# The two gates of a recurrent block: from two block-diagonal products to two products in row halves

## The chip, the cores and the metric

The kernel runs on one core of a Trainium2 chip. The metric is the time on the device of one execution, in microseconds, as the median of the runs shown. The core has a matrix engine (TensorE, PE in the profile), two engines for element-wise work (VectorE, DVE, and ScalarE, ACT), a general engine (GpSimd, POOL) and a queue engine that issues the transfers (SP).

## What is computed

A two-layer transformer block for 256 latent and 256 context tokens (T = 512 in all) of width 1024, in float32. Each layer has a feed-forward part, a mixer with three branches (a recurrent one, one with a matrix state, called ml below, and an attention), and another feed-forward part, all modulated by a conditioning vector. The change sits in the recurrent branch, whose gates are:

```python
def rglru_coeffs(u, wa, ba, wi, bi, lam):
    ...
    ub = u.reshape(B, L, RNN_BLOCKS, RNN_BLOCK)
    r = jax.nn.sigmoid(jnp.einsum('blni,nij->blnj', ub, wa).reshape(B, L, D_RNN) + ba)
    i = jax.nn.sigmoid(jnp.einsum('blni,nij->blnj', ub, wi).reshape(B, L, D_RNN) + bi)
    log_a = -LRU_C * jax.nn.softplus(-lam) * r
    a = jnp.exp(log_a)
    b = jnp.sqrt(-jnp.expm1(2.0 * log_a)) * (i * u)
    return a, b
```

There are 8 blocks of 64 features (512 in all), each with its own 64 x 64 matrix for each of the two gates r and i, and all of this for each of two directions d of the scan that follows. The input u is the result of a short convolution.

## The kernel before

Features lie on the 128 partitions, the 512 tokens along the row, so the 512 recurrent features are four chunks c of 128, each with two blocks of 64. `rg_scan` (line 702) works on one chunk after another. It loads the chunk's gate weights (line 706) and convolves (`conv`), both one chunk ahead, then goes over the two directions. Per direction it makes two products, one for each gate g, each with a 128 x 128 matrix that holds the two 64 x 64 blocks on its diagonal and zeros elsewhere (line 732), and each followed by a tanh on ScalarE that brings the product from its PSUM bank to SBUF as tr or ti (line 733; the sigmoid is made from a tanh). Then ScalarE makes q and e from tr (lines 742 and 743) and VectorE the rest of the coefficients (lines 744 to 747). At the end of a chunk come, for both directions, a square root on ScalarE (line 757), a product and a scan on VectorE. The program names are u (input), rgw (weights), rg (the bank of a product), ba (bias).

The recurrent branch is one of three chains of small steps (`rg_scan`, `mlstm` and `attend`) that run beside the large products pj of the mixer's input projection. These are made by `mm3` from weights split in a high and a low part: lines 261, 262 and 263 are its three products, line 246 (cast, ScalarE, whi) and line 247 (difference, VectorE, wlo) make the parts. `tick`, called between halves of the large products, takes the next step of each chain at a fixed rate per microsecond of large products. TensorE so works in the order of the program text; the order of ScalarE and VectorE is made by a scheduler from priorities and dependences. Two or three of the eight PSUM banks serve the large products here, the others the chains.

Other names below: vf (line 1105) is a copy on ScalarE of a projected value, which TensorE then transposes into vt (line 1110); p (lines 877 and 883 on ScalarE, 876 and 884 on VectorE) are decay factors and weighted scores of ml, used by the product av (line 903); st (line 861) are its scores, ht (line 935) turns its output; rot (line 1247) turns the queries of the attention; ssq (line 1257) sums squares in four column groups; asq, aq and to (lines 1138, 1142 and 1128) are further evacuations of projections on ScalarE.

Of the kernel before, what the change touches and what calls it, by code (L numbers as in the profile page):

```python
# [16 lines left out]
P = 128  # L17
# [22 lines left out]
# steps of the side chains per microsecond of large products, by layer  # L40
# [8 lines left out]
# columns of the constant array  # L49
# [10 lines left out]
# columns of the per-layer vectors  # L60
V_G = 0            # 3 x 8 x 2
V_ADAB = 48        # 72 x 2
V_CW = 192         # 4 chunks x 4 taps
V_CB = 208
V_BA = 212         # d x c
V_BI = 220
# [5 lines left out]
V_SINK = 243       # 8  # L72
# [4 lines left out]
# projection chunks of w_in in the order in which they are used  # L77
# [6 lines left out]
def body(ctx, tc, ins, out):  # L84
# [29 lines left out]
    def give(n):  # L114
        """n more slots for weights (or fewer, n < 0)"""
        for _ in range(n):
            free[0].append(free[1].pop(0))
        for _ in range(-n):
            free[1].append(free[0].pop())

# [15 lines left out]
    def pgive(n):  # L136
        """n more banks for the large products (or fewer, n < 0)"""
        a, b = (1, 0) if n > 0 else (0, 1)
        for _ in range(abs(n)):
            banks[b].append(banks[a].pop(0))  # L140

    # ---- small work that runs beside the large products. The tensor engine works in the order of this program:
    # what needs it waits for the end of a large product, so that its operands are there when its turn comes ----
# [4 lines left out]
    def defer(n, f):  # L148
        """call f after n large products"""
        later.append([n, f])  # L150

    def start(gen, rate):
        """a chain of steps; rate: steps per microsecond of large products"""
# [86 lines left out]
    def split_w(r, n):  # L240
        """[128, n] weights, chunks of 128 rows side by side -> float32r parts in tiles of 4 chunks"""
# [13 lines left out]
    def mm3(ps, w, kk, xh, xl, cols, ks=None, koff=0):  # L255
        """ps[:, cols] (+)= w.T x in float32 accuracy: high x high + high x low + low x high"""
# [8 lines left out]
    def mm3_beside(ps, w, kk, xh, xl, cols):  # L265
        """the same, with a place for small work in the middle; the caller ticks the second half"""
# [5 lines left out]
    def split_act(src, cols=BOTH, name="y"):  # L272
        """float32 data in two float32r slots"""
# [10 lines left out]
    def ada_load(h):  # L284
        """a quarter of the weights of the first two modulations, by chunk of the contraction"""
# [10 lines left out]
    def ada_first(w, ps, ks):  # L296
        """their products on the idle tensor engine, four column groups at once"""
# [24 lines left out]
    def ada_second():  # L322
        """the next modulation on the tensor engine, in steps"""
# [29 lines left out]
    def cond_load():  # L353
        """silu of both conditioning vectors, on every partition"""
# [14 lines left out]
    def ada_steps():  # L369
        """the modulations: features on partitions, sums along the rows of the turned weights"""  # L370
# [8 lines left out]
        for i, (l, m) in enumerate(ADA_MODS):  # L379
            # nothing reads the last of the second layer's for the second stream  # L380
# [31 lines left out]
    def rsqrt(v, shape):  # L412
        """v ** -0.5 of a small tile: a first guess from the exponent bits, then Newton steps"""
# [41 lines left out]
    def norm_rstd(s, use, lag=2):  # L455
        """use(rows of 1 / rms on all partitions), some large products later"""
# [42 lines left out]
    # the first chunks of a projection from h, in the order in which h comes: the columns, the chunks of the  # L499
    # contraction, and how many chunks of features take turns  # L500
# [35 lines left out]
    def passes_of(streams, load, use, ahead=None, begin=None):  # L536
        """the products that end a part: the last chunks stream by stream, so that the next norm of one runs beside
# [1024 lines left out]
```

## Time and profile before

| what | value |
|---|---|
| median of 3 runs | 2230.23 us (2229.87 to 2230.32) |
| profiled execution, first to last instruction | 2228.2 us |
| TensorE busy | 2186.7 us |
| VectorE busy | 1495.2 us |
| ScalarE busy | 1021.4 us |
| gate products, first start and last start | 455.9 and 1805.2 us |

The profiled execution has no time of its own beside its span; the runs' median is 2.0 us above the span. In a view in order of time each line is a start, a duration, an engine, a line of the kernel, an operation with its output and inputs, and in brackets the idle time before it and what ended that. Ends of products on TensorE are modelled and overlap the next start, so the cost of a product is read from start to start. A group of products on one line of the view ("x4") can hold several instructions.

### The profile page before, as it was taken

Reading aid. Unit: us, or ns where it says so; the run is one execution under the profiler, and the core shown is the slowest. Engines: PE = TensorE matmul, PEld = TensorE weight load, DVE = VectorE, ACT = ScalarE, POOL = GpSimd, SP = SyncE. Lnnn points to the kernel's source line nnn. Section 1 sums busy time; section 2 is a strip of 40 time slices with the busy share of each in tenths; the row PEclk is TensorE's granted clock in tenths of the full one; section 3 lists DMA queues with packets and bytes.
Section 4 is the critical chain, followed back from the end, with each engine's and each line's share of the span. In section 5 each row is a group of like instructions: output and inputs, shape, how many; then the busy total and the mean of one; then the engine's idle time right before and its main releaser. Section 6 shows DMA issues by size and latency. Waiting matters only on the chain.

```text
span 2228.2 us, 32885 instructions
## 1 busy us (share of the span) xinstructions
PE 2186.7 (98%) x12357; PEld 1856.5 (83%) x12357; DVE 1495.2 (67%) x3605; ACT 1021.4 (46%) x2021; POOL 4.7 (0%) x40
## 2 busy tenths in 40 slices
PE   6999999999999999999999999999999999998999
PEld 5778888977877778998888898888889778998999
DVE  5899834679766645689973368754346987776664
ACT  4322223468575534542222353232335887655553
POOL 0000000000000000000000000000000000000000
PEclk9999999999999999999999999999999999999999
DMA  9665522311111322445552226642222222454552
GB/s 357 227 236 209 188 92 102 109 62 64 65 57 67 114 86 95 152 160 211 210 175 103 77 89 238 247 165 95 88 93 87 88 83 97 141 181 178 209 189 86
DMA packets 74944, 310.30 MB, mean 139 GB/s; under 512 B 7072, under 2 KB 10656, under 8 KB 60704
## 3 DMA queue, kind: packets, MB, share of 16 engines
q1 hardware_dynamic: 74784, 308.19, 39.0%
q8 instruction: 97, 1.59, 0.3%
q14 instruction: 63, 0.52, 0.1%
HBM read 303.97 MB, written 4.19 MB: 138 GB/s over the span
## 4 chain that ended last, share of the span: by engine, by line
PE 91%; DVE 4%; ACT 3%; DMA 1%; issue 1%; SPq 0%; ACTq 0%; DVEq 0%
PE p L261 11%; PE p L262 11%; PE p L263 11%; PE dn L261 6%; PE dn L262 6%; PE dn L263 6%; PE pg L262 3%; PE pg L261 3%; PE pg L263 3%; PE pj L261 3%; PE pj L262 3%; PE pj L263 3%; PE up L261 2%; PE up L262 2%; PE up L263 2%; PE ao L998 1%
## 5 line engine op out<-in xcount | busy, mean ns | idle before, releaser
L246 ACT CAST whi<-raw 128x512 fp32r<-128x512 f32 (+1 forms) x844 | 506.7, 612 | 830.9 <-PE p L262 385.4
L247 DVE TENSOR_TENSOR wlo<-raw,whi 128x512 fp32r<-128x512 f32 (+1 forms) x844 | 564.2, 678 | 362.0 <-ACT whi L246 352.5
L261 PE MATMUL p<-hh,whi 128*128 128x512 f32 (+1 forms) x1216 | 445.4, 366 | 0.5 <-ACT silu L579 0.5
L262 PE MATMUL p<-hl,whi 128*128 128x512 f32 (+1 forms) x1216 | 445.6, 366 | 0.0
L263 PE MATMUL p<-hh,wlo 128*128 128x512 f32 (+1 forms) x1216 | 444.0, 365 | 0.0
L387 DVE SCALAR_TENSOR_TENSOR junk<-ada,cb 128x512 f32<-128x512 f32 x416 | 290.0, 697 | 34.8 <-DMA ada<-ada 27.7
L261 PE MATMUL dn<-gh,whi 128*128 128x512 f32 (+1 forms) x809 | 275.6, 341 | 0.0
L263 PE MATMUL dn<-gh,wlo 128*128 128x512 f32 (+1 forms) x809 | 275.1, 340 | 0.0
L262 PE MATMUL dn<-gl,whi 128*128 128x512 f32 (+1 forms) x809 | 274.9, 340 | 0.0
L261 PEld LDWEIGHTS p<-hh,whi 128*128 128x128 f32 x1216 | 228.4, 188 | 43.1 <-issue 1.2
L263 PEld LDWEIGHTS p<-hh,wlo 128*128 128x128 f32 x1216 | 228.5, 188 | 40.4
L262 PEld LDWEIGHTS p<-hl,whi 128*128 128x128 f32 x1216 | 228.5, 188 | 39.6
L262 PEld LDWEIGHTS dn<-gl,whi 128*128 128x128 f32 x809 | 152.2, 188 | 18.8
L261 PEld LDWEIGHTS dn<-gh,whi 128*128 128x128 f32 x809 | 152.2, 188 | 18.7
L263 PEld LDWEIGHTS dn<-gh,wlo 128*128 128x128 f32 x809 | 152.1, 188 | 18.7
L261 PE MATMUL pj<-hh,whi 128*128 128x512 f32 (+1 forms) x400 | 153.8, 384 | 1.2 <-DVE li L776 1.2
L262 PE MATMUL pj<-hl,whi 128*128 128x512 f32 (+1 forms) x400 | 143.9, 360 | 0.0
L263 PE MATMUL pj<-hh,wlo 128*128 128x512 f32 (+1 forms) x400 | 143.5, 359 | 0.0
L262 PE MATMUL pg<-hl,whi 128*128 128x512 f32 (+1 forms) x384 | 129.9, 338 | 0.0
L261 PE MATMUL pg<-hh,whi 128*128 128x512 f32 (+1 forms) x384 | 129.8, 338 | 0.0
L263 PE MATMUL pg<-hh,wlo 128*128 128x512 f32 (+1 forms) x384 | 129.3, 337 | 0.0
L496 DVE SCALAR_TENSOR_TENSOR x<-dn,Ga,x 128x256 f32<-128x256 f32 x168 | 74.8, 479 | 54.1 <-PE dn L263 53.4
(281 smaller groups left out, 3444.5 us busy)
## 6 DMA issues: line engine op xcount, KB each, us to landing
raw<-w SPq DMA_DIRECT2D x104, 1024.0 KB, 4.8
ada<-ada SPq DMA_DIRECT2D x124, 512.0 KB, 3.8
raw<-win SPq DMA_DIRECT2D x30, 1024.0 KB, 4.8
raw<-w SPq DMA_DIRECT2D x32, 896.0 KB, 4.6
raw<-wbr SPq DMA_DIRECT2D x24, 1024.0 KB, 4.8
raw<-wbo SPq DMA_DIRECT2D x24, 512.0 KB, 3.3
raw<-wout SPq DMA_DIRECT2D x8, 1024.0 KB, 4.7
raw<-ada SPq DMA_DIRECT2D x6, 1024.0 KB, 6.4
```

Source lines behind the costliest of these rows:

```text
L246: S.copy(hi[:, :e], r[:, a:a + e])
L247: V.tensor_tensor(lo[:, :e], r[:, a:a + e], hi[:, :e].bitcast(F32), op=ALU.subtract)
L261: PE.matmul(o, hi[:, ws], xh[k][:, cols], start=(k == 0), stop=False)
L262: PE.matmul(o, hi[:, ws], xl[k][:, cols], start=False, stop=False)
L263: PE.matmul(o, lo[:, ws], xh[k][:, cols], start=False, stop=(k == kk - 1))
L387: V.scalar_tensor_tensor(junk[0], r[:, e * T:(e + 1) * T], 1.0, cb[2 * s + e][:, :T], op0=ALU.mult, op1=ALU.mult, accum_out=am[:, b, s, e: ...
L496: V.scalar_tensor_tensor(x[k][:, c], ps[:, c], Gate[l, n][:, k, s:s + 1], x[k][:, c], op0=ALU.mult, op1=ALU.add)
L998: PE.matmul(po[c][rows, cc], vts[0][:, sv * P + 64 * hf:sv * P + 64 * hf + 64], pt[s // 2][:, (s % 2) * 256:(s % 2) * 256 + 256], start=(s ...
```

## The change

Per direction there are still two products of 512 columns, but now one for each block b of 64 features and not for each gate. The 64 rows of weights of a block hold its two matrices side by side (64 x 128, the first gate in columns 0 to 63, the second in 64 to 127). The first product uses the upper 64 rows of the array, the second the lower 64, with the matching 64 rows of u. So a bank holds the two gates of one block, one above the other, where before it held one gate of two blocks. Since the gates are needed by gate on 128 partitions, four tanh of 64 rows take the place of two of 128: each reads one half of a bank and writes one half of tr or ti, two of the four into other partitions than they read. Both banks are held until the fourth. The weights of a chunk shrink from 128 x 512 to 128 x 256, and the bias columns are laid out by block and direction. The diff, without the lines that only drop comments:

```diff
-            nc.sync.dma_start(w[:, :T], ins["rgw"][l, c])
+            nc.sync.dma_start(w[:, :TL], ins["rgw"][l, c])
...
-                for g, t in ((0, tr), (1, ti)):
-                    ps = palloc("rg")
-                    PE.matmul(ps, rgw[:, (2 * d + g) * P:(2 * d + g + 1) * P], u, start=True, stop=True)
-                    S.activation(t[:, :T], ps, AF.Tanh, scale=0.5,
-                                 bias=ba2[l][:, 8 * g + dc:8 * g + dc + 1])
-                    pfree(ps)
+                pss = [palloc("rg") for _ in range(2)]
+                for b, ps in enumerate(pss):
+                    r = slice(64 * b, 64 * b + 64)
+                    PE.matmul(ps, rgw[r, d * P:(d + 1) * P], ut[r, :T], start=True, stop=True)
+                for b, ps in enumerate(pss):
+                    for g, t in ((0, tr), (1, ti)):
+                        S.activation(t[64 * b:64 * b + 64, :T], ps[64 * g:64 * g + 64, :], AF.Tanh, scale=0.5,
+                                     bias=ba2[l][64 * g:64 * g + 64, 2 * dc + b:2 * dc + b + 1])
+                pfree(*pss)
...
-    rgw = np.zeros((DEPTH, 4, P, 2, 2, P), np.float32)
+    rgw = np.zeros((DEPTH, 4, 2, 64, 2, 2, 64), np.float32)
...
-                s = slice(64 * b, 64 * b + 64)
                 for d in range(2):
-                    rgw[l, c, s, d, 0, s] = f["rg_wa"][l, d, 2 * c + b]
-                    rgw[l, c, s, d, 1, s] = f["rg_wi"][l, d, 2 * c + b]
+                    rgw[l, c, b, :, d, 0] = f["rg_wa"][l, d, 2 * c + b]
+                    rgw[l, c, b, :, d, 1] = f["rg_wi"][l, d, 2 * c + b]
...
-        v[:, V_BA:V_BA + 8] = col(f["rg_ba"][l].reshape(-1))
-        v[:, V_BI:V_BI + 8] = col(f["rg_bi"][l].reshape(-1))
+        v[:, V_BA:V_BA + 16] = np.concatenate([f["rg_ba"][l].reshape(16, 64), f["rg_bi"][l].reshape(16, 64)], 1).T
...
-    o.update(win=win, wbr=wbr, wbo=wbo, wout=wout, rgw=rgw.reshape(DEPTH, 4, P, 512), vec=vec)
+    o.update(win=win, wbr=wbr, wbo=wbo, wout=wout, rgw=rgw.reshape(DEPTH, 4, P, 256), vec=vec)
```

The order of TensorE's instructions is the same before and after. ScalarE has 1963 instead of 1931 instructions, 53 table loads in both; its order changes in the stretches of the mixers. Two places in the second layer, with line numbers of the kernel in question (after the change lines 733, 742, 757, 877, 883, 1105, 1115, 1128 and 246 are lines 735, 744, 759, 879, 885, 1107, 1117, 1130 and 245).

ScalarE, second layer, where the copy vf for the first value head stands; before:

```order
L883 ACTIVATE p_15589<-mb_15554,gt_15521 128x256
L883 ACTIVATE p_15592<-mb_15554,gt_15521 128x256
L757 ACT_TABLE_LOAD
L757 ACTIVATE q_15546<-q_15546 128x512
L1105 COPY vf_15577<-pj_15533 128x512
L733 ACT_TABLE_LOAD
L733 ACTIVATE tr_15579<-rg_15581,ba_1_112 128x512
L733 ACTIVATE ti_15580<-rg_15584,ba_1_112 128x512
L742 ACTIVATE q_15641<-tr_15579,sp_1_110 128x512
L1115 COPY v_2884_15623<-vt_15618 128x4x128
```

and the same place after the change:

```order
L885 ACTIVATE p_15613<-mb_15576,gt_15543 128x256
L885 ACTIVATE p_15616<-mb_15576,gt_15543 128x256
L245 CAST whi_15688<-raw_15619 128x512
L245 CAST whi_15779<-raw_15777 128x512
L1107 COPY vf_15599<-pj_15555 128x512
L735 ACTIVATE tr_15601<-rg_15603,ba_1_112 64x512
L735 ACTIVATE ti_15602<-rg_15603,ba_1_112 64x512
L735 ACTIVATE tr_15601<-rg_15604,ba_1_112 64x512
L735 ACTIVATE ti_15602<-rg_15604,ba_1_112 64x512
L744 ACTIVATE q_15665<-tr_15601,sp_1_110 128x512
L745 ACTIVATE e_15666<-tr_15601,sp_1_110 128x512
```

The square root q of the chunk ahead and its table load stood ahead of vf and stand behind it now, and with them the table load of the tanh is gone from here; two casts whi stand ahead of vf, and four tanh behind it.

ScalarE, the exponentials p ahead of the product av, some ten instructions later; before:

```order
L883 ACTIVATE p_15651<-mb_15554,gt_15521 128x128
L246 CAST whi_15753<-raw_15751 128x512
L246 CAST whi_15757<-raw_15751 128x512
L757 ACT_TABLE_LOAD
L757 ACTIVATE q_15641<-q_15641 128x512
L877 ACT_TABLE_LOAD
L877 ACTIVATE p_15656<-p_15656 128x128
L877 ACTIVATE p_15698<-p_15698 128x128
L877 ACTIVATE p_15702<-p_15702 128x128
L883 ACTIVATE p_15702<-mb_15554,gt_15521 128x128
```

and after the change:

```order
L885 ACTIVATE p_15675<-mb_15576,gt_15543 128x128
L1130 ACTIVATE to_15662<-pj_15629 128x256
L759 ACT_TABLE_LOAD
L759 ACTIVATE q_15568<-q_15568 128x512
L879 ACT_TABLE_LOAD
L879 ACTIVATE p_15680<-p_15680 128x128
L759 ACT_TABLE_LOAD
L759 ACTIVATE q_15665<-q_15665 128x512
L879 ACT_TABLE_LOAD
L879 ACTIVATE p_15722<-p_15722 128x128
L879 ACTIVATE p_15726<-p_15726 128x128
L885 ACTIVATE p_15726<-mb_15576,gt_15543 128x128
```

The two casts have gone ahead, and the square root of the chunk ahead, with its table load and one more load for the exponential behind it, stands between the first exponentials and the last.

## Rows read from the trace of the kernel before

**Rows 1.** the page, busy time of each engine

```profile
PE 2186.7 (98%) x12357; PEld 1856.5 (83%) x12357; DVE 1495.2 (67%) x3605; ACT 1021.4 (46%) x2021; POOL 4.7 (0%) x40
```

**Rows 2.** the page, the chain that ended last, by engine

```profile
PE 91%; DVE 4%; ACT 3%; DMA 1%; issue 1%; SPq 0%; ACTq 0%; DVEq 0%
```

**Rows 3.** busy us (instructions) of PE, PEld, DVE, ACT, POOL; clock; DMA; two stretches

```profile
455.00:549.00 94.00, 94.00 (x403) 70.26 (x402) 83.18 (x193) 76.28 (x138) 0.27 (x3) 1.00 0.21 72
1745.00:1805.00 60.00, 56.21 (x310) 44.62 (x309) 58.83 (x141) 52.28 (x97) 0.23 (x3) 1.00 0.28 93
```

**Rows 4.** waits in 1720 to 1810: engine, line, waited for, total, times, longest

```profile
DVE wlo L247 <- ACT whi L246: 1.4, 2, 0.8
...
PE ht L935 <- ACT hv L929: 1.2, 1, 1.2
PE vt L1110 <- ACT vf L1105: 1.1, 1, 1.1
...
PE rg L732 <- DVE p L884: 0.9, 1, 0.9
...
PE av L903 <- DVE p L884: 0.5, 1, 0.5
```

**Rows 5.** shapes of line 732: count, duration ns min/median/max, first and last start

```profile
L732 PE MATMUL rg<-u,rgw x64: 590/592/697, 455.9 to 1805.2; 128*128 128x512 f32 x64
```

**Rows 6.** TensorE in time, a pair of gates (start, us, engine, line)

```profile
455.68 0.39 PE L263 MATMUL pj<-hh,wlo 128*128 128x512 f32 x1
455.91 1.88 PE L732 MATMUL rg<-u,rgw 128*128 128x512 f32 x4
...
457.86 0.39 PE L262 MATMUL pj<-hl,whi 128*128 128x512 f32 x1
```

**Rows 7.** TensorE in time, four column groups (ssq) among full products

```profile
549.38 0.59 PE L861 MATMUL st<-q,k 128*128 128x256 f32 x2
549.91 1.06 PE L1257 MATMUL ssq<-asq,con 128*32 128x512 f32 x8
...
551.24 0.40 PE L262 MATMUL pj<-hl,whi 128*128 128x512 f32 x1
```

**Rows 8.** TensorE in time, products over 32 rows among full ones

```profile
558.54 0.24 PE L1267 MATMUL ssqd<-con,ssqk 32*128 32x32 f32 x1
558.71 0.33 PE L1266 MATMUL ssqc<-con,ssqr 128*128 128x128 f32 x1
558.97 0.24 PE L1267 MATMUL ssqd<-con,ssqk 32*128 32x32 f32 x1
```

**Rows 9.** shapes of line 1301 on ScalarE, columns as in rows 5

```profile
L1301 ACT CAST k2h<-aq x8: 613/618/622, 576.6 to 1828.4; 64x512 fp32r<-64x512 f32 x8
```

**Rows 10.** shapes of line 246 on ScalarE, columns as in rows 5

```profile
L246 ACT CAST whi<-raw x844: 499/620/658, 24.2 to 2206.3; 128x512 fp32r<-128x512 f32 x156, 128x384 fp32r<-128x384 f32 x13
```

**Rows 11.** ScalarE in time, a pair's tanh

```profile
1734.62 0.68 ACT L733 ACTIVATE tr<-rg,ba 128x512 f32<-128x512 f32 x1
1735.19 0.69 ACT L733 ACTIVATE ti<-rg,ba 128x512 f32<-128x512 f32 x1
```

**Rows 12.** ScalarE in time, a square root ahead of the copy vf

```profile
1753.72 1.28 ACT L757 ACT_TABLE_LOAD   x1 [0.75 <-DVE e L746]
1755.02 0.63 ACT L757 ACTIVATE q<-q 128x512 f32<-128x512 f32 x1
1755.55 0.57 ACT L1105 COPY vf<-pj 128x512 f32<-128x512 f32 x1
```

**Rows 13.** ScalarE in time, the exponential ahead of av

```profile
1766.25 0.35 ACT L883 ACTIVATE p<-mb,gt 128x128 f32<-128x128 f32 x1
```

**Rows 14.** ScalarE in time, the copy vf of layer 0

```profile
492.72 0.57 ACT L1105 COPY vf<-pj 128x512 f32<-128x512 f32 x1
```

**Rows 15.** TensorE in time, the product on that copy

```profile
494.17 0.60 PE L1110 MATMUL vt<-con,vf 128*128 128x128 f32 x4
```

**Rows 16.** transfers by line: name, queue, count, size, us to landing

```profile
rgw<-rgw SPq DMA_DIRECT2D x8, 256.0 KB, 2.6
```

More of the change, by code (lines that the diff above doesn't have):

```diff
@@ L65 @@
 V_BA = 212
-V_BI = 220
 V_LAM = 228
```

## The prediction

> **What bounds the kernel now.** I read the busy times first, then the chain of work that ended last, then the places where the changed products stand, then the waits around them. TensorE is busy for 2186.7 of 2228.2 us [rows 1], and it holds 91% of the chain; VectorE holds 4% and ScalarE 3% [rows 2]. So a product taken away shortens the kernel, as long as the work between two products, on ScalarE and VectorE, keeps up. The changed lines sit in two stretches only, the recurrent gates of layer 0 (455 to 549 us) and of layer 1 (1720 to 1807 us). In the first, TensorE is busy for all 94.00 of 94 us, ScalarE for 76.28 and VectorE for 83.18; in the second, between 1745 and 1805, TensorE is busy for 56.21 of 60 us, VectorE for 58.83 and ScalarE for 52.28 [rows 3]. The reader should see that these are two different stages: in layer 0 TensorE never waits, in layer 1 VectorE is all but full and TensorE already waits for ScalarE and VectorE: for ht 1.2, vt 1.1, rg 0.9 and av 0.5 us, 3.7 us in all [rows 4]. A saving on TensorE passes through in the first kind of stage and is swallowed in the second.
>
> **What the change removes on TensorE.** Before, a direction of a chunk has two products of 128 x 128 weights; the trace has 64 records for 2 layers x 4 chunks x 2 directions x 2 gates, so a product is two records, and there are 16 pairs of products [rows 5]. What a pair costs is read from starts, because the ends overlap: the first record of a pair starts at 455.91, and the second large product behind the pair starts at 457.86; that is 1.95 us, less one large product (455.68 to 455.91, 0.23 us), so 1.72 us for four records, 0.43 each [rows 6]. After the change a pair is again two products of 512 columns, but each over 64 rows of weights, one in the upper and one in the lower half of the array. If the halves work side by side, two rounds of 0.43 remain, 0.86 us.
>
> What entering and leaving the half-row form costs is not in the trace of before for this shape. The nearest row is work in four column groups: st starts at 549.38 and its two records of 256 columns take as long as one of 512 (0.43), so the column groups begin at 549.81; the second large product behind them starts at 551.24; 1.43 less 0.23 is 1.20 us for eight records, which one after the other would be 3.43 [rows 7]. Four groups do run abreast: two rounds, 0.86, and 0.34 over for going in and out. Another row is work over 32 rows only, small, between full products: the starts stand 0.17 to 0.26 us apart [rows 8], so a change of form is of the order of 0.1 to 0.2 us there and not of a microsecond. I take 0.34, and 0.08 more because the weights loaded at the entry are 128 columns wide instead of 32 (a guess of a size, inside the bounds). The new pair is then 0.86 + 0.34 + 0.08 = 1.28, and I round to a saving of 0.45 a pair: 16 x 0.45 = **7.2 us**, 3.6 in each layer. The bounds: no cost of going in and out, 0.86, saves 16 x 0.86 = 13.7 us; halves that do not run abreast, 1.72 + 0.42 = 2.14, lose 16 x 0.42 = 6.7 us. I take 0.45 since the column groups show both things at once, groups abreast and a price for them, at the same 512 columns and type.
>
> A page speaks against the change here: the Trainium skill, "TensorEngine Tiling (Array Packing)", section Key Properties, says that a change of the tiling mode, not merely of the tile, drains TensorE. The trace agrees as far as 0.34 us of boundary goes [rows 7]; without the rule the sum on TensorE would be 13.7 us instead of 7.2.
>
> **What it adds on ScalarE.** The two evacuations of 128 x 512 become four of 64 x 512. A cast of 64 x 512 has a median of 618 ns [rows 9] beside 620 for 128 x 512 [rows 10], so the time goes with the columns and halving the rows saves nothing. Before, the two tanh stand 0.57 us apart (1734.62 and 1735.19) [rows 11]. So a pair has 2 x 0.57 = 1.14 us more on ScalarE: 9.1 us in each layer, 18.2 in all. Could it be less? Only if an instruction on 64 rows were shorter, which the two casts deny; more, if writing to other rows than are read cost something, for which no row exists; I take nothing for it, and what it would cost is inside R3. Layer 0 has 94 - 76.28 = 17.7 us free on ScalarE in that stretch and takes 9.1 of it. In layer 1 the stretch 1745 to 1805 holds five pairs, 5.7 us, on 7.7 free. A share of 58 of 60 leaves nearly no slack at any place.
>
> **What follows for the order.** TensorE's order stays the same; its products only meet other moments. The order of ScalarE is made out new between the gates and the rest, and this moves the places where TensorE waits in layer 1, as the order listings ahead show. (A) Before, a square root with its table load (1753.72 to 1755.55, 1.83 us) stands ahead of the copy vf [rows 12], and vt waits 1.1 us for that copy [rows 4]. After, this piece stands behind vf; in its place come two casts (2 x 0.6 = 1.2 [rows 10]), and two more tanh of the pair ahead (1.14) have to fit in as well, for which there are the 0.75 us that ScalarE waits at 1753.72 [rows 12]. So vf comes 1.83 - 1.2 = 0.6 us earlier, or, where the tanh use up more than the idle time, 0.3. I take 0.6. (B) Before, av waits 0.5 us [rows 4] for exponentials of which the last on ScalarE starts at 1766.25 [rows 13]. The piece taken out at (A), with the table load that follows vf in the listing (another 1.28, as at 1753.72; 1.83 + 1.28 = 3.1 us) [rows 12], comes back right ahead of these, so that here only the additions count: two tanh more of this pair and two of the pair ahead, 2.28, less the 0.75 of idle time, 1.5 at most; and with some of the casts gone behind, 0.4 at least. I put the exponentials 0.7 to 1.0 us later. Then the waits for p before rot and rg (0.9 in the row of rg [rows 4]) grow by 1 to 2 us, because VectorE, 58.83 of 60, can't make up a delay. Against that the last two pairs, where TensorE is fully busy again, give 0.9. In sum: vf -0.6, av and what follows +1.9, last pairs -0.9: layer 1 comes to **+0.4 us**, gain and loss cancelling.
>
> In layer 0 the slack is what decides: vf starts at 492.72 and takes 0.57, and vt needs it at 494.17, 0.9 us of slack, the tightest that I found for ScalarE [rows 14, 15]. With 3.6 us given back and 1.14 us more on ScalarE per pair, a stall or two of half a microsecond should turn up. I take 1.0: **-2.6 us** for layer 0.
>
> **What costs nothing.** The gate weights are 128 KB per chunk instead of 256; a load of 256 KB lands after 2.6 us [rows 16] and is issued while the chunk ahead of it is worked on, so it hides before and after. PSUM: a pair took one bank and then another, each given back after its tanh; now both are held until the fourth tanh, 0.57 and 1.14 us longer. Who is waiting for such a bank are products of the two mixers (st, rot), which come later anyway; that delay is within the ±1 of layer 1 above. The waits that TensorE has more of are for products at least 17 instructions back, which are done. The bias columns are only placed otherwise. The queues of the DMAs and of the fifth engine keep their order.
>
> **The sum.** -2.6 + 0.4 = -2.2 us. The profiled span is 2228.2 us and the median of the runs 2230.23; the 2.0 us between them lie around the span and aren't touched. So 2230.2 - 2.2 = **2228.0 us**. About 0.2%, 4.5 us, is what a measurement of this kernel can tell from no change: this forecast is below it.
>
> **Rivals.**
> R1, the forecast: the saving on TensorE passes in layer 0 and is swallowed in layer 1. It gives 2226 to 2231.
> R2, the saving passes through in both layers: ScalarE's added tanh fall into its idle time, the waits of 3.7 us [rows 4] stay as they are. For it: in the whole stretch VectorE waits 1.4 us for casts [rows 4] and TensorE not at all, so ScalarE has something to postpone. Against it: VectorE's 58.83 of 60 [rows 3]. It gives 2230.2 - 7.2 = 2223.0, to 2217 if the boundary is free.
> R3, slower: ScalarE sets the pace in layer 1. Its idle time before was 7.7 us of 60, much of it waiting for a partner; if this can't be used, each of the eight added pairs of tanh is on the path: 8 x 1.14 = 9.1, less 2.6 from layer 0, so 2236.7. It decides once the free 7.7 us are bound by waits for VectorE rather than free. Against it: casts can move by microseconds.
> R4, the halves don't do what the change needs. If the second product's first record may start only once the first product's second record has started, three rounds are left, 3 x 0.43 + 0.42 = 1.71: no gain, and some 2231.5 with the added tanh. If they run one after the other, 2.14, the loss is 6.7 and more: 2238. The column groups [rows 7] speak against both. A page would have the first: the Trainium skill, "TensorE: Matmul & The Clock Gate", section Part 3: Packing small matmuls (The mechanism), says that products start and end in the program's order. The trace does not agree for the column groups, whose eight records would then need five rounds, 2.15 us, and take 1.20 [rows 7]; row halves of 512 columns it does not show.
>
> **How the numbers follow.** R1 0.56, R2 0.24, R3 0.10, R4 0.10 (0.06 the overlapped, 0.04 the serial one). Faster by over 0.2% is R2: 0.24. Within 0.2%: R1 and the overlapped R4, 0.62. Slower by over 0.2%: R3 and the serial R4, 0.14. The range holds R1, the overlapped R4 and the nearer three quarters of R2: 2222.5 to 2232.5, 0.80. The far part of R2, R3 and the serial R4 are left out.
>
> **What would show it.** In the profile after: a pair from start to start, less one large product, at 1.2 to 1.35 us (1.7 or 2.1 by R4, 0.9 with a free boundary); four tanh 0.57 us apart; in layer 0 no waits of TensorE over 1 us and a stretch shorter by some 2.6; in layer 1 a wait of vt below 1.1 and one of av or rot above 0.5 to 1.5, with the stretch as long as before. The prediction is wrong if a tanh of 64 rows takes clearly less than 0.5 us, if a pair costs over 1.6, or if layer 1 gets shorter by 3 us: then ScalarE had room that I don't see.

## The result, and the profile after

The changed kernel takes 2242.1 us (median of 4 runs, 2240.93 to 2243.09) beside 2230.28 for the kernel before: a ratio of 1.0053, with a 95% interval of 1.0039 to 1.0067. It is 12 us slower. The forecast was 2228.0, in a range up to 2232.5. The profiled span is 2241.3 us, 13.1 more than before.

The page of the changed kernel, its busy times and the chain that ended last:

```profile
PE 2187.1 (98%) x12357; PEld 1852.2 (83%) x12357; DVE 1496.0 (67%) x3605; ACT 1046.3 (47%) x2053; POOL 4.7 (0%) x40
...
PE 89%; ACT 5%; DVE 4%; DMA 1%; issue 1%; SPq 0%; ACTq 0%
```

These answer [rows 1, 2]. TensorE is as busy as before (2187.1 and 2186.7 us), although 16 pairs of products became shorter: part of its work ran at half the clock, as shown below. ScalarE has 24.9 us more (1046.3 and 1021.4) and 5% of the chain, where it had 3%.

The two stretches of [rows 3], with the same columns (busy us of PE, PEld, DVE, ACT, POOL, then the clock):

```profile
455.00:549.00 94.00, 91.42 (x399) 66.30 (x398) 79.91 (x188) 83.63 (x145) 0.27 (x3) 0.98 0.17 59
1745.00:1805.00 60.00, 47.04 (x256) 36.45 (x253) 53.82 (x124) 53.87 (x96) 0.23 (x3) 0.92 0.21 73
```

In layer 0 TensorE has lost 2.6 us of its 94, in layer 1 it is down from 56.21 to 47.04 of 60, and the granted clock, 1.00 before in both, is 0.98 and 0.92. The products themselves did what was forecast. TensorE in time, the first pair (start, us, engine, line):

```profile
456.53 0.40 PE L262 MATMUL pj<-hh,wlo 128*128 128x512 f32 x1
456.86 1.13 PE L732 MATMUL rg<-u,rgw 64*128 64x512 f32 x4
...
458.26 0.40 PE L261 MATMUL pj<-hl,whi 128*128 128x512 f32 x1
```

From 456.53 to 458.26 are 1.73 us; less two large products of 0.23 the pair costs 1.27, where it cost 1.72 before [rows 6]. The four records start at 456.859 and 456.866, and 457.393 and 457.399, two and two abreast. The tanh did not. ScalarE in time, one pair's four tanh and the next instruction:

```profile
1758.10 0.69 ACT L735 ACTIVATE tr<-rg,ba 64x512 f32<-64x512 f32 x1
1758.81 0.69 ACT L735 ACTIVATE ti<-rg,ba 64x512 f32<-64x512 f32 x1
1759.52 0.69 ACT L735 ACTIVATE tr<-rg,ba 64x512 f32<-64x512 f32 x1
1760.23 0.68 ACT L735 ACTIVATE ti<-rg,ba 64x512 f32<-64x512 f32 x1
1760.94 0.82 ACT L744 ACTIVATE q<-tr,sp 128x512 f32<-128x512 f32 x1
```

They stand 0.71 us apart, not 0.57 [rows 11]: each begins 0.02 us after the one before has ended, while two tanh of 128 rows overlap by 0.11. Four take 2.84 us, two took 1.14; a pair has 1.70 us more on ScalarE, not 1.14.

Where TensorE stood still: the waits from 445 to 565 us, and from 1720 to 1830, in the form of [rows 4] (engine, line, waited for, total, times, longest).

```profile
PE pj L262 <- DVE wlo L246: 2.2, 1, 2.2
...
```

```profile
PE pj L262 <- DVE wlo L246: 5.5, 2, 5.3
...
PE av L905 <- DVE p L886: 3.3, 2, 2.9
...
```

Before, TensorE waited only once from 445 to 565 us, 1.2 us for li at 446, ahead of the gates; that wait is still there. In layer 1 the four waits of [rows 4] sum to 3.7 us; now there are eight groups of waits, which sum to 14.4. Three single waits are of a new size: 2.2 us at 505, 2.9 (of the 3.3 for av) at 1770 and 5.3 at 1798. Behind each the clock falls. Busy times and clock (the third column from the right) around the three of them:

```profile
505.00:508.00 3.00, 0.81 (x5) 0.38 (x4) 3.00 (x6) 2.98 (x7) 0.00 (x0) 1.00 0.00 0
...
509.00:512.00 3.00, 3.00 (x8) 1.69 (x7) 2.44 (x9) 2.90 (x6) 0.00 (x0) 0.50 0.40 112
...
1772.00:1778.00 6.00, 5.38 (x18) 3.68 (x18) 3.11 (x11) 5.91 (x11) 0.00 (x0) 0.50 0.00 0
...
1798.00:1803.00 5.00, 0.00 (x0) 0.00 (x0) 5.00 (x12) 4.35 (x9) 0.00 (x0) 0.95 0.00 0
1803.00:1809.00 6.00, 5.84 (x14) 3.65 (x14) 3.92 (x9) 1.50 (x4) 0.00 (x0) 0.50 0.38 118
```

From 505 to 508 TensorE works 0.81 of 3 us; the granted clock goes to 0.50, which is 1.2 GHz, from 509 to 512, although TensorE is busy again throughout, and is back at 1.00 from 514 on. Behind the wait for av it is at 0.50 from 1772 to 1778. From 1798 to 1803 it does nothing, and from 1803 to 1809 it runs at 0.50 again. At that level a large product takes 0.43 us from start to start and not 0.23.

### The profile page after: what moved, and what is told of

It is laid out like the page before. It is cut to its first block, busy times and chain, and to the rows that moved or that the text cites. A ratio compares the mean times of both kernels' runs of the same rounds, so it can differ in the third digit from the quotient of the medians.

```text
span 2241.3 us, 32931 instructions
## 1 busy us (share of the span) xinstructions
PE 2187.1 (98%) x12357; PEld 1852.2 (83%) x12357; DVE 1496.0 (67%) x3605; ACT 1046.3 (47%) x2053; POOL 4.7 (0%) x40
## 4 chain that ended last, share of the span: by engine, by line
PE 89%; ACT 5%; DVE 4%; DMA 1%; issue 1%; SPq 0%; ACTq 0%
PE p L260 11%; PE p L261 11%; PE p L262 11%; PE dn L260 6%; PE dn L261 6%; PE dn L262 6%; PE pg L261 3%; PE pg L260 3%; PE pg L262 3%; PE pj L260 2%; PE pj L262 2%; PE pj L261 2%; PE up L260 2%; PE up L261 2%; PE up L262 2%; PE ao L1000 1%
```

## Experiments

To tell where the 12 us come from, the change is taken apart into three: the products, the tanh, and the order of ScalarE's and VectorE's instructions, which the scheduler makes anew. The order of TensorE is one and the same in all kernels of the table. The table gives the ratio to the kernel before, which ran beside each group, and, from one profile each, how much longer than before it takes from the start of the first pair to the start of the last pair of each layer (91.8 and 79.5 us before). The last pair itself, 0.45 us shorter with halves, is not in it.

| run | products | tanh a pair | order | ratio (95%) | layer 0 | layer 1 |
|---|---|---|---|---|---|---|
| prod_only | halves | 2 of 128 | before | 0.9988 (0.9978 to 0.9997) | -2.0 | +0.1 |
| order_of_after | full | 2 of 128 | after | 1.0027 (1.0017 to 1.0036) | 0.0 | +5.2 |
| tanh_only | full | 4 of 64 | after | 1.0041 (1.0026 to 1.0056) | +1.1 | +9.2 |
| order_of_before | halves | 4 of 64 | before | 1.0043 (1.0028 to 1.0058) | +2.8 | +7.0 |
| changed kernel | halves | 4 of 64 | after | 1.0053 (1.0039 to 1.0067) | +1.5 | +12.2 |

### The products alone

```diff
-                for b, ps in enumerate(pss):
-                    for g, t in ((0, tr), (1, ti)):
-                        S.activation(t[64 * b:64 * b + 64, :T], ps[64 * g:64 * g + 64, :], AF.Tanh, scale=0.5,
-                                     bias=ba2[l][64 * g:64 * g + 64, 2 * dc + b:2 * dc + b + 1])
+                for b, t in ((0, tr), (1, ti)):
+                    S.activation(t[:, :T], pss[b], AF.Tanh, scale=0.5, bias=ba2[l][:, 2 * dc + b:2 * dc + b + 1])
```

> The products of the changed kernel (two over 64 rows each) with two tanh of 128 x 512 per direction as before, so the gates stay mixed by block and the output is not the reference's. ScalarE's and VectorE's order is that of the kernel before, instruction for instruction. Theory (the loss comes from the four tanh, not from the products): a pair costs 1.27 us from start to start and the kernel is 4 to 7 us faster than before, 2223 to 2226, granted clock 0.997 as before. Rival (work in row halves itself brings the clock down, or the saving is swallowed by the waits of layer 1): 2228 to 2236, with stretches of granted clock 0.5 behind the pairs.

Measured: 0.9988, 2.7 us faster, clock 0.997 over the span. That is less than the 4 to 7 expected, and as a time (2228.7 us) it lies at the lower end of the rival's span. Of the rival's two causes one is out: row halves don't bring the clock down, it is at 1.00 from 455 to 549 and from 1720 to 1830. The other holds for layer 1: the gain is in layer 0 (-2.0, some -2.5 with its last pair) and is all but absent in layer 1 (+0.1, some -0.4 with the last pair). The waits in layer 1, from 1720 on:

```profile
PE rt L828 <- DVE r L819: 1.7, 1, 1.7
...
PE vt L1110 <- DVE u L716: 1.6, 1, 1.6
...
PE ht L935 <- ACT hv L929: 1.2, 1, 1.2
PE av L903 <- DVE p L884: 1.2, 1, 1.2
```

With 0.7 for rg these sum to 6.4 us, where those of [rows 4] sum to 3.7: most of what TensorE saves there it waits for. This is what the forecast said of the two stages.

### The tanh alone

```diff
-                for g, t in ((0, tr), (1, ti)):
-                    ps = palloc("rg")
-                    PE.matmul(ps, rgw[:, (2 * d + g) * P:(2 * d + g + 1) * P], u, start=True, stop=True)
-                    S.activation(t[:, :T], ps, AF.Tanh, scale=0.5, ...)
-                    pfree(ps)
+                pss = [palloc("rg") for _ in range(2)]
+                for g, ps in enumerate(pss):
+                    PE.matmul(ps, rgw[:, (2 * d + g) * P:(2 * d + g + 1) * P], u, start=True, stop=True)
+                for b, ps in enumerate(pss):
+                    for g, t in ((0, tr), (1, ti)):
+                        S.activation(t[64 * b:64 * b + 64, :T], ps[64 * g:64 * g + 64, :], AF.Tanh, scale=0.5, ...)
+                pfree(*pss)
```

> The products of the kernel before with four tanh of 64 x 512 per direction, each reading and writing the rows that the changed kernel reads and writes, both banks held to the fourth; the gates are mixed by block, so the output is not the reference's. ScalarE's and VectorE's order is that of the changed kernel. Theory (the four tanh and what the scheduler makes of them cost all of it): slower than before by 12 to 18 us, 2242 to 2248, with waits of TensorE for wlo and p in the same three places and the clock at 0.5 behind each. Rival (the tanh cost little, the products did it): 2229 to 2234.

Measured: 1.0041, 9.1 us slower, less than the 12 to 18 expected. Two of the three stalls are there, from 1720 on:

```profile
PE pj L263 <- DVE wlo L247: 5.4, 2, 5.3
...
PE av L905 <- DVE p L886: 2.8, 1, 2.8
```

The one in layer 0 is 0.8 us here: with products of 1.72 us TensorE comes to that place later (507.4 us, not 505.6), while the wlo that it waits for is ready at about the same time. So the shorter products turned their saving into a longer wait there. The clock falls only behind the 5.3 us, not in all three places as expected: behind the 2.8 us for av it stays at 1.00, where in the changed kernel it is at 0.50 from 1772 to 1778 behind 2.9 us. From tanh_only to the changed kernel the shorter products gained nothing that can be measured; the intervals of the two overlap.

### The order alone, both ways

In each of these two kernels the order of one stands on the work of the other: on ScalarE and on VectorE each instruction (got) is bound behind the one that the list (seq) has ahead of it, which sets their order and makes no wait (the traces have the bound order, instruction for instruction):

```diff
+        for a, b in zip(seq, seq[1:]):
+            tc.add_manual_dep(got[b], got[a].name, info, reason="order")
```

> The kernel before, nothing changed in its work, with ScalarE's and VectorE's instructions in the order that they have in the changed kernel (a pair's tanh where its later half stands). Theory 1 (the new order is what costs: wlo and the exponentials stand behind the square roots and scans): slower than before by 6 us or more, 2236 to 2244. Theory 2 (the longer tanh cost, the order is the scheduler's fit to them): 2229 to 2234.

> The changed kernel in full, with ScalarE's and VectorE's instructions in the order of the kernel before (the two halves of a tanh one behind the other in its place). Theory 1 (the order costs): 2224 to 2232, waits of TensorE under 1.5 us each, clock 0.997. Theory 2 (the four tanh cost 0.70 us each, 1.66 more for a pair, on engines that are full): 2236 to 2243, with the wait for wlo at 505 us and in layer 1 as before the exchange.

Measured: the old work in the new order is 1.0027, 6.0 us slower, as theory 1 had it; the new work in the old order is 1.0043, 9.6 us slower, as theory 2 had it, though without the long wait for wlo that theory 2 named as its sign. So neither theory holds alone. The new order costs by itself, all of it in layer 1 (+5.2) and there in one place, as the waits of order_of_after from 1720 on show:

```profile
PE pj L267 <- DVE wlo L251: 5.5, 2, 5.3
...
PE av L907 <- DVE p L888: 0.8, 1, 0.8
```

This is the stall of 5.3 us, and TensorE has it whatever the tanh cost. VectorE around that wlo, first in the kernel before, then in the changed kernel, whose order this is:

```profile
1789.42 0.68 DVE L247 TENSOR_TENSOR wlo<-raw,whi 128x512 fp32r<-128x512 f32 x1
1790.02 0.69 DVE L758 TENSOR_TENSOR ti<-ti,q 128x512 f32<-128x512 f32 x1
...
1790.96 1.22 DVE L763 TENSOR_TENSOR_SCAN q<-e,ti 128x512 f32<-128x512 f32 x1
```

```profile
1797.94 0.67 DVE L760 TENSOR_TENSOR ti<-ti,q 128x512 f32<-128x512 f32 x1
...
1798.78 1.21 DVE L765 TENSOR_TENSOR_SCAN q<-e,ti 128x512 f32<-128x512 f32 x1
...
1802.42 0.69 DVE L246 TENSOR_TENSOR wlo<-raw,whi 128x512 fp32r<-128x512 f32 x1
```

Eight instructions that stood behind this wlo before now stand ahead of it: a product with a square root, a scan and six others. From the first of them to the wlo, 1797.94 to 1802.42, are 4.5 us, all but 0.6 of it theirs; in order_of_after it is 4.5 us as well. But the old order doesn't save the changed kernel either. With it the long stall is gone and twelve groups of short waits, 14.6 us in all, stand in its place, from 1720 on in order_of_before:

```profile
PE av L909 <- DVE p L890: 1.9, 2, 1.5
...
PE rot L1253 <- ACT ti L739: 1.6, 1, 1.6
...
```

Against prod_only, which has the same order and the same products, the four tanh cost 9.6 + 2.7 = 12.3 us. ScalarE has 16 x 1.70 = 27.2 us more work there, so a little under half of it reaches the end. Some of it may come by way of the banks: rot doesn't read ti, so what it waits 1.6 us for must be a bank that the tanh gives back, and st waits 1.3 us in the same way. No run takes this apart from the length of the tanh.

### How much tanh it takes

The same gates can be had with four products of 64 x 64 that use all quarters of the array. Without more, the second gate's blocks lie exchanged, and two crossed tanh put them right, so there are three in a pair:

```diff
+                for g in range(2):
+                    for b in range(2):
+                        r = slice(64 * b, 64 * b + 64)
+                        o = r if g == 0 else slice(64 - 64 * b, 128 - 64 * b)
+                        PE.matmul(pss[g][o, :], rgw[r, d * P + 64 * g:d * P + 64 * g + 64], ut[r, :T], ...)
+                S.activation(tr[:, :T], pss[0], AF.Tanh, scale=0.5, bias=ba2[l][:, dc:dc + 1])
+                for b in range(2):
+                    r, o = slice(64 * b, 64 * b + 64), slice(64 - 64 * b, 128 - 64 * b)
+                    S.activation(ti[r, :T], pss[1][o, :], AF.Tanh, scale=0.5, bias=ba2[l][o, 8 + dc:9 + dc])
```

> The same four products without the copy of u: the second gate's blocks then lie exchanged in their bank, and are put right by two crossed tanh of 64 x 512; the first gate keeps one of 128 x 512. Order of ScalarE and VectorE as before. Three tanh: 0.57 + 2 x 0.71 = 1.99 us a pair between 1.14 (prod_only, -2.7 us) and 2.84 (order_of_before, +9.6 us). Theory (the time follows what the tanh take on ScalarE): halfway, +1 to +6 us, 2231 to 2238 on a chip with before at 2232. Rival (a step: either hidden whole or not): within 1.5 us of one of the two.

Measured: 1.0008 (0.9999 to 1.0018), 1.8 us slower, in the expected span and no step. The three stand 0.70 to 0.71 us apart, the one of 128 rows too, since the next works on 64; that is 2.1 us a pair. With the old order throughout, 1.14, 2.1 and 2.84 us of tanh a pair give -2.7, +1.8 and +9.6 us: the first 1.0 us more costs 4.5, the next 0.7 us 7.8. (The products of tanh_three are those of the quarters, a pair some 0.04 us shorter than in halves; the intervals are some 2 us to either side, 3 for the last.)

### Why a tanh of 64 rows stands further from the next

```diff
+                for b, g in ((0, 0), (0, 1), (1, 0), (1, 1)) if l == 0 else ((0, 0), (1, 0), (0, 1), (1, 1)):
+                    r = slice(64 * b, 64 * b + 64)
+                    S.activation((tr, ti)[g][r, :T], pss[g][r, :], AF.Tanh, scale=0.5, ...)
```

> The products of the kernel before and four tanh of 64 x 512 that write the rows that they read; in layer 0 two on the lower half follow each other, then two on the upper, in layer 1 the halves alternate. Order of ScalarE and VectorE as in the changed kernel, so that it stands beside tanh_only, where the rows are crossed. Theory 1 (an instruction on 64 rows doesn't overlap the next, whatever the rows): 0.71 us from start to start in both layers, time as tanh_only, +9 us. Theory 2 (crossing the halves is what costs): 0.57 in both, time as order_of_after, +5 us. Theory 3 (a change of the half costs): 0.57 behind the first of each two in layer 0, 0.71 elsewhere.

Measured: the third theory, in ScalarE's times. Layer 0, upper half after upper half (459.40 to 459.99), then the next instruction on all rows; and layer 1, where the halves alternate (x2 is two instructions):

```profile
459.40 0.68 ACT L739 ACTIVATE tr<-rg,ba 64x512 f32<-64x512 f32 x1
459.99 0.67 ACT L739 ACTIVATE ti<-rg,ba 64x512 f32<-64x512 f32 x1
460.69 0.82 ACT L748 ACTIVATE q<-tr,sp 128x512 f32<-128x512 f32 x1
```

```profile
1727.07 1.38 ACT L739 ACTIVATE tr<-rg,ba 64x512 f32<-64x512 f32 x2 [0.48 <-PE rg L736]
1728.47 1.38 ACT L739 ACTIVATE ti<-rg,ba 64x512 f32<-64x512 f32 x2
```

In layer 0 the second tanh on the same half follows after 0.59 us, while one on the other half, or an instruction on all rows, follows after 0.68 to 0.70; in layer 1 all four stand about 0.70 apart. So what is lost is the overlap of one instruction's end with the next one's start, and it is lost where the rows change. The changed kernel's four tanh change their rows at every step, in what they read or what they write. The time of this run is 1.0042, as tanh_only: it saves some 0.25 us of ScalarE on a pair in layer 0 and next to none in layer 1.

### What the clock costs

```diff
+            for _ in range({(0, CH_ATQ): 8, (1, CH_ATV): 21}.get((l, ci), 0)):
+                PE.matmul(ps[:, cols], w[0][0][:, 0:P], hh[0][:, cols], start=True, stop=True)
             mm3_beside(ps, w, KD, hh, hl, cols)
```

> The changed kernel in its own order with idle products put in front of the two units whose third product waits for wlo: 8 of 128 x 512 in layer 0 (at 505 us, where TensorE waits 2.2 us) and 21 in layer 1 (at 1797, 5.3 us). They write the bank that the unit then overwrites. Theory (the stall is one cost and the halved clock behind it another): the stretches at 0.5 behind these two places go, the stall's end stays, and the kernel is 3 to 5 us faster than the changed one, ratio to before 1.003 instead of 1.0053. Rival (VectorE sets the pace behind the stall anyway, the clock costs nothing): the same as the changed kernel within 1 us.

Measured: 1.0029 (1.0018 to 1.0041), where the changed kernel has 1.0053 (1.0039 to 1.0067): some 5 us come back, as the theory had it, though the two intervals just touch. TensorE in time around the second place (L1161 are the idle products), and the clock behind it:

```profile
1795.68 4.74 PE L1161 MATMUL pj<-hh,whi 128*128 128x512 f32 x20
...
1801.35 0.50 PE L266 MATMUL pj<-hh,wlo 128*128 128x512 f32 x1 [0.47 <-DVE wlo L250]
1801.69 0.39 PE L264 MATMUL pj<-hh,whi 128*128 128x512 f32 x1
1801.92 0.39 PE L265 MATMUL pj<-hl,whi 128*128 128x512 f32 x1
```

```profile
1801.00:1804.00 3.00, 2.65 (x12) 1.94 (x14) 3.00 (x8) 1.15 (x4) 0.00 (x0) 1.00 0.00 0
...
```

TensorE still waits 0.47 us for wlo at 1801.35, so the stall has its old end; but then it goes on at 0.23 us a product, with a granted clock of 1.00, where it went at 0.43. Between the profiles, layer 0 is 1.2 and layer 1 is 2.8 us shorter than in the changed kernel, 4.0 in all. The third stall, ahead of av, was left as it was.

### A version that keeps two tanh

If the second gate's products read a copy of u with its halves exchanged, they can use the two free quarters and yet leave both gates in place; then two tanh of 128 rows are enough. Two transfers from SBUF to SBUF make the copy, a chunk ahead:

```diff
+            us = salloc("us")
+            for b in range(2):
+                nc.sync.dma_start(us[64 * b:64 * b + 64, :T], u[64 - 64 * b:128 - 64 * b, :T])
...
+                for g, x_ in ((0, ut), (1, us)):
+                    for b in range(2):
+                        r = slice(64 * b, 64 * b + 64)
+                        k = r if g == 0 else slice(64 - 64 * b, 128 - 64 * b)
+                        PE.matmul(pss[g][r, :], rgw[k, d * P + 64 * g:d * P + 64 * g + 64], x_[k, :T], ...)
```

> Four products of 64 x 64 weights per direction, one in each quarter of the array, so that each gate lands in its own bank, block 0 above block 1, and two tanh of 128 x 512 are enough again. The second gate's products sit in the other row half than their block, so they read a copy of u with its halves exchanged, made by two transfers of 64 x 512 from SBUF to SBUF, a chunk ahead. ScalarE and VectorE keep the order of the kernel before. Theory (the loss was all in the four tanh): the pair costs 1.3 us as in prod_only, 2 to 4 us faster than before (ratio 0.9985), the gain in layer 0 and none in layer 1. Rival 1 (four quarters don't run abreast): a pair at 1.7 to 2.2 us and 0 to 7 us slower. Rival 2 (the transfers hold up the weight loads behind them in SP's queue): a wait for wlo or whi that isn't there before, slower by 2 us or more.

Measured: 1.0009 (1.0000 to 1.0017), 2 us slower, against the theory; and it was neither rival. The waits from 440 to 460 us show a third thing:

```profile
PE pj L264 <- DVE li L786: 3.5, 1, 3.5
```

Before, this wait was 1.2 us. The copy takes one more slot of SBUF, and so the next chunk's u came to lie in a slot that the last products of the stage before still read. VectorE stood at that convolution, which began at 446.82 us and not at 442.94, and li behind it. (The clock fell here too, to 0.59 on the mean of 452 to 455.) The next kernel puts the copy in the slot of the padded input xp, which is free by then; all else is the same:

```diff
-            sfree(xps[c])
-            us = salloc("us")
+            us = xps[c]
```

> quad_swapped_u with the exchanged copy of u in the slot of the padded input xp, which is free once the convolution has read it, so that no later tile moves to another slot. In quad_swapped_u the second chunk's u came to lie in a slot that a product still read, VectorE waited there and li behind it, and TensorE lost 3.5 us at 450 us. Theory (that loss was the slot): no wait for li over 1.5 us, and the gain of prod_only comes out, 2 to 4 us faster than before, ratio 0.9982 to 0.9992. Rival (the transfers or four tiles cost it): as quad_swapped_u, 1.0009.

Measured: 0.9979 (0.9970 to 0.9988), 2225.97 us beside 2230.3: 4.3 us faster than before, a little more than expected, and faster than both kernels. A pair in TensorE's time, and the busy times of its page:

```profile
466.02 0.65 PE L740 MATMUL rg<-u,rgw 64*64 64x512 f32 x2
466.04 0.65 PE L740 MATMUL rg<-xp,rgw 64*64 64x512 f32 x2
466.50 0.59 PE L740 MATMUL rg<-u,rgw 64*64 64x512 f32 x2
466.52 0.60 PE L740 MATMUL rg<-xp,rgw 64*64 64x512 f32 x2
467.04 0.63 PE L811 MATMUL fr<-con,z 128*64 128x128 f32 x4
```

```profile
PE 2178.8 (98%) x12421; PEld 1847.1 (83%) x12421; DVE 1494.2 (67%) x3605; ACT 1019.3 (46%) x2021; POOL 4.7 (0%) x40
```

From 466.02 to 467.04, two rounds of about 0.5 us hold eight records, and TensorE is busy for 7.9 us less than before, while ScalarE and VectorE have what they had. The wait for li is 1.2 us again, as before the change. In layer 0 it gains 1.9 us, in layer 1 it loses 0.2; the last pair of each layer, which this leaves out, gives some 0.5 more each time, so that 2.7 us are accounted for. The rest lies where the kernels don't differ, and one profile of each can't resolve it.

> The same with ScalarE and VectorE in the order that the scheduler makes for it; against the order of before, 27 places of 1896 on ScalarE and 89 of 3189 on VectorE differ. Theory (an order made without the true times is worth some us either way, as order_of_after showed with 5 to 6): between 2 us faster and 4 us slower than quad_in_xp. Rival (so few moves do nothing): within 1 us of it.

Measured: 0.9983 (0.9974 to 0.9992), 0.7 us behind quad_in_xp, within the rival's 1 us, and within the theory's span as well. So few moves do nothing that can be measured here.

## Why the prediction was wrong, point by point

**TensorE's saving: right.** 1.28 us were forecast for a pair and 1.27 measured, and R4 falls. In part this is luck: the forecast was two rounds of 0.43 and 0.42 for going in and out, and the trace has two rounds of 0.53 and some 0.1 at either end. The guessed 0.08 for wider weights no run shows by itself.

**Two stages: right in kind, and the likeness of the sizes is luck.** prod_only shows the saving passing in layer 0 (some -2.5 with the last pair) and nearly swallowed in layer 1 (some -0.4). That this is close to "-2.6 for layer 0" and "+0.4" proves nothing: those sums had 1.0 and 1.9 us of stalls from the tanh and the order in them, which prod_only doesn't have; without these stalls layer 0 should have given 3.6. The changed kernel itself has +1.5 and +12.2.

**The term that failed: "2 x 0.57 = 1.14 us more on ScalarE".** It is 1.70. The step took the 618 ns of a cast of 64 rows [rows 9] as the same as 620 for 128 [rows 10], and from it that a tanh of 64 rows has a pitch of 0.57 too. But a duration is not a pitch. Two instructions of 128 rows overlap by 0.11 us, two of 64 rows on other halves don't. Of writing to other rows than are read the prediction said "I take nothing for it"; it costs this overlap, and so does a mere change of the half (tanh_rows). On TensorE the prediction had read costs from start to start, on ScalarE it didn't.

**The larger error: what the tanh do to the time.** Even at 0.57 each they would have been 18.2 us of new work, and the working let a net 1 us of stall in layer 0 and some 2 in layer 1 stand for them. This is the step that failed most: measured by order_of_before against prod_only, four tanh cost 12.3 us. The sentence "A share of 58 of 60 leaves nearly no slack at any place" was right, and what followed from it was R3, which gave 2236.7 and had a chance of 0.10; even R3 had layer 0 gain 2.6 us, where it loses 1.5. The chain in layer 0 shows how it goes; VectorE in time, in the kernel before and then in the changed one, ahead of the first stall:

```profile
495.90 0.69 DVE L744 SCALAR_TENSOR_TENSOR ti<-ti,u 128x512 f32<-128x512 f32 x1 [0.54 <-ACT ti L733]
...
498.17 0.69 DVE L745 SCALAR_TENSOR_TENSOR ti<-e,ti 128x512 f32<-128x512 f32 x1 [0.20 <-ACT e L743]
...
505.30 3.09 DVE L247 TENSOR_TENSOR wlo<-raw,whi 128x512 fp32r<-128x512 f32 x5
```

```profile
497.46 0.69 DVE L746 SCALAR_TENSOR_TENSOR ti<-ti,u 128x512 f32<-128x512 f32 x1 [2.19 <-ACT ti L735]
...
500.48 0.69 DVE L747 SCALAR_TENSOR_TENSOR ti<-e,ti 128x512 f32<-128x512 f32 x1 [0.68 <-ACT e L745]
...
507.07 3.09 DVE L246 TENSOR_TENSOR wlo<-raw,whi 128x512 fp32r<-128x512 f32 x5
```

VectorE waits 2.19 us for ti and 0.68 for e, where before it waited 0.54 and 0.20, and so the five wlo start at 507.07 and not at 505.30; before, TensorE never stood here. The prediction took vf for the tightest place of layer 0 [rows 14, 15], which is ScalarE's own, and did not follow what VectorE does behind the gates. A page names the copy out of PSUM as a risk: the Trainium skill, "TensorEngine Tiling (Array Packing)", section PSUM Bottleneck, says that after a fourfold gain on TensorE it may become the bottleneck. The trace agrees in direction with a much smaller gain: products 0.45 us a pair shorter, and here the tanh that copy 1.70 us longer as well.

**The order was followed on the wrong engine.** The listings were of ScalarE, and places (A) and (B) were weighed to about a microsecond. The 5.3 us stand on VectorE, at a wlo that was moved behind eight other instructions; order_of_after shows that the new order as a whole costs 6.0 us with no other change, and this stall is nearly all of it. At (A) nothing was gained: vt waits 1.1 us there as before, and what comes last is now p on VectorE. Of (B) the direction was right: the exponentials were put 0.7 to 1.0 us later, and av waits 2.9 us at once, where it waited 0.5.

**The banks.** Under "What costs nothing" the longer hold of the banks was put within the ±1 of layer 1. In the changed kernel that is so, rot waits 0.9 us for a bank of the tanh; in the old order (order_of_before) it is not, rot and st wait 2.9 us. Nor is the first bank held to the fourth tanh: rot starts at 1789.99, when the second has ended at 1789.93, the last of the four to read that bank.

**Not in the prediction at all: the clock.** A stall was priced at its own length. Three stalls of over 2 us each were followed by at least 3, 6 and 6 us at 1.2 GHz, and clock_fill shows some 5 us for two of them. The Trainium skill, "TensorE: Matmul & The Clock Gate", section HAM oscillation, says that a wait of TensorE can bring its clock to the lower level, so that the work behind the wait starts slow; the trace agrees with 0.50 behind 5.3 us of standing still, and the prediction should have weighed it.

**What stays open.** How the 12 us of the changed kernel divide between order, tanh and clock isn't a sum: the order alone costs 6.0, the tanh in the new order 3.1 more, the halves 2.7 more, but the tanh in the old order 12.3. The 3.1 and the 2.7 are within the intervals of their runs. What each costs depends on the others. Whether an order fitted to the true pitch of the tanh would have let the changed kernel keep its gain wasn't tried.

## What to carry to other kernels

A saving on a full engine that is bought with work on its neighbours has to be priced on the neighbours: count the instructions there, read their cost from start to start with the same rows and the same neighbours, and follow the engine behind them, not only the one that runs them. A stall can cost more than its length, if the clock falls behind it. If a product can be put where its result is needed, by using another part of the array and a copied input whose transfers nothing waits for, the gain can come without the bill, as in quad_in_xp.

## What the runs showed of the hardware

- Consecutive ScalarE instructions overlap by about 0.11 us only while they work on the same rows: 0.57 to 0.59 us from start to start on the same half or on all 128 rows, 0.68 to 0.71 where the half changes or is crossed, or where 64 and 128 rows follow each other (tanh, 512 columns, float32, out of PSUM).
- Products in row halves and in quarters of the array run abreast in float32: two records with 128 columns of weights, or four with 64, in a round of about 0.5 us (0.53 and 0.48 from start to start).
- TensorE's clock fell to 0.50 behind single waits of 2.2, 2.9, 3.5 and 5.3 us, and was at 1.00 throughout these two stretches of the kernel before, whose longest wait there is 1.2 us. The length of a wait alone does not decide: in tanh_three the clock fell behind waits of 2.0 and 1.9 us and stayed at 1.00 behind one of 2.2 between them; in tanh_only it stayed at 1.00 behind 2.8 us; in order_of_before it fell behind two waits of 0.8 and 1.0 us that stand 0.7 us apart. What else decides no run here shows.
